# Weight sums of layer B's output blocks made in the attention passes, and two smaller moves beside them

## The chip, the cores and the metric

The kernel runs on one core of a Trainium2 chip, in one launch. The metric is the time of one execution on the device in microseconds (us), as the median of several executions. Lower is better. Five engines share the core: TensorE (PE in the profile, with PEld for its weight loads), VectorE (DVE), ScalarE (ACT), GpSimd (POOL) and SyncE (SP), which issues nearly all DMAs of this kernel. Each engine works through its own list of instructions in order, so an instruction that waits holds up all that stands behind it on that engine.

## The reference

Two layers, each with a gated attention, over a prompt of 2048 rows and a sample of 64 rows, 1024 features wide, all in float32. Layer B, the second, matters here:

```python
def gated_attention_layer(x_p, x_s, ck, cv, norm_g, w_in, q_g, k_g, w_out,
                          n_heads, n_kv, past_chunks, bias_fn, sinks):
    qp, kp, vp, gp = project(x_p, norm_g, w_in, q_g, k_g, n_heads, n_kv)
    op = prompt_band_attention(qp, kp, vp, past_chunks, bias_fn, sinks)
    y_p = x_p + (op * jax.nn.silu(gp)) @ w_out
    ...
    os_, nk, nv = sample_band_attention(qs, ks, vs, ck, cv, bias_fn, sinks)
    y_s = x_s + (os_ * jax.nn.silu(gs)) @ w_out
```

The change touches how the last product, `(op * silu(gp)) @ w_out` of layer B, gets its weights.

## The kernel before

Every float32 operand of a large product is split into a high part (rounded by ACT, `xh` or `wh`) and the rest (`xl` or `wl`, by DVE or POOL), and a product is three matmuls: high by high, high by low, low by high. A split of one 128x512 piece is therefore one ACT instruction and one DVE or POOL instruction.

The program is one long row of projection *jobs* (class `Filler`), into which the attention of both layers is woven by hand: PE's order is written out by the program. The order on the other engines and on SP is made by a scheduler that works with estimated times. Small pieces of work that nobody waits for at once (weight splits, norms) go into a queue (`Background`); it is drained a few items at a time beside the attention. When a job starts, it prefetches the activations of the next one and may start the weights of a later one (`Filler.step`).

Layer A comes first, then its output projection, then layer B in eight *passes* (two heads each, `hp` 0 to 7), each over the units 0 to 6, 8 (the sample) and 7. What follows the passes is the place of this change:

- **The direct jobs.** The first 512 rows of the layer's output are projected directly: `output_jobs(1, 1, ...)` for the right half of the columns and `output_jobs(1, 0, ...)` for the left, two jobs each of 256 rows, 96 matmuls a job. They stand beside the attention of the last units. Each job runs over four column blocks `m`; two of them share a residual tile `res` (two buffers in all), which is loaded from `x1`, added to the product by DVE (L1481) and stored to `y` (L1485). The eight weight chunks of a half come through three buffers `wraw`; each is split by ACT (L329) and DVE (L330), and the eighth of the left half into four small tiles `ev` (L739, L740).
- **The blocks.** The other 1536 rows are three blocks of 512 rows (`block_output`). Each is a 2x2 block product done with seven products instead of eight (a Strassen-Winograd scheme): products 0, 1, 2 use weights as they are, products 3 to 6 use sums of weight blocks named `t2`, `t3`, `t1` and `t4`. Each product has 48 matmuls. Product 0 is copied from PSUM to the tile `p1` by ACT (L1689), and product 1 then adds to the same PSUM banks, so PE may start product 1 only behind that copy. Between the first block's product 1 and product 2 stands the sample's output, `work(1)` and `work(0)` (L1520 to L1530).
- **The sums before.** `run` (inside `block_output`) first issues the loads of the weight blocks into tiles `R` (L1557), and makes the sums there: four DVE instructions for each of four slices `k` (L1564, L1565, L1569, L1570), twelve splits into tiles `tw` (ACT L1573, POOL or DVE L1575) and four of `t4` (ACT L1582, POOL L1583). The tiles of `block_output` lie where the attention's tiles were, so nothing of this can start before the attention's last outputs.

The operands of product `g` are made two products ahead (`operand`, splits at L1640 and L1642, sums at L1631 to L1635); the products' results are added to the residual tiles `R` by DVE and POOL (L1674).

Of the kernel before, what the change touches and what calls it, by code (L numbers as in the profile page):

```python
# [15 lines left out]
P = 128  # L16
# [35 lines left out]

DT = 256
ATTENTION = {
    "p", "ph", "pl", "q1", "G", "gt", "o1", "pa", "pb", "sq", "f", "nm", "sm", "VT", "VS",
# [4 lines left out]
def hybrid_encoder_kernel(  # L60
# [179 lines left out]
    x1 = dr.tile([P, KC, TOK], F32, tag="x1", name="x1")  # L240
    xs = dr.tile([P, 2 * KC * TOK], F32, tag="xsa", name="xsa")
    xo = dr.tile([P, 4 * NU + 1, 8 * P], F32, tag="xo", name="xo")

# [544 lines left out]
    class Filler:  # L788
# [9 lines left out]
        def step(self):  # L798
            if self.gen is None:
                self.n += 1  # L800
                if self.n >= len(self.jobs):
                    return False
                if self.n == 0:
                    self.x = self.jobs[0].prefetch()
                    self.jobs[0].weights()
                for q in self.x.items:
                    bg.run(q)
                if self.n + 1 < len(self.jobs):
                    nxt = self.jobs[self.n + 1]
                    self.x = nxt.prefetch()  # L810
                    if nxt.weights is not None:
                        nxt.weights()
                if self.n + EARLY < len(self.jobs):
                    nxt = self.jobs[self.n + EARLY]
                    if nxt.weights is not None and nxt.early:
                        nxt.weights(WP)
                self.gen = self.jobs[self.n].gen()
            c = next(self.gen, None)
            if c is None:
                self.gen = None  # L820
                return self.step()
            self.done += c
            if not self.attending:
                bg.drain(FR * c)
            return True
# [335 lines left out]
    def layer_b():  # L1161
# [226 lines left out]
        def pipeline():  # L1388
# [8 lines left out]
            filler.attending = True  # L1397
            prev = pend = None
            for x, it in enumerate(its):
                heads = [(i, h) for h in range(2) for i in range(len(it.unit[2]))]  # L1400
                c0 = filler.done
# [42 lines left out]
    def output_jobs(layer, half, xin, xout, W, count, early=True, small=-1):  # L1444
# [8 lines left out]
        def add_unit(j):  # L1453
# [9 lines left out]
            def gen():  # L1463
                oc = st.x.pop(j)
                w = st.w
                for m in range(4):
                    if m % 2 == 0:
                        c = 4 * half + m
                        res = t("res", [P, 2 * OT], 2)
                        rv = res[:, : 2 * W].rearrange("p (k s) -> p k s", k=2)  # L1470
                        load(rv, xin[:, c : c + 2, o : o + W])
                    ps = psum("pj", 512, 2)
                    for k in range(KC):
# [5 lines left out]
                        if k < KC - 1:  # L1479
                            yield 3 * W / 2400  # L1480
                    nc.vector.tensor_tensor(rv[:, m % 2], ps[:, :W], rv[:, m % 2], op=ALU.add)  # L1481
                    if "sq" in held:
                        held.pop("sq")()
                    if m % 2:
                        store(xout[:, c : c + 2, o : o + W], rv)  # L1485
                        if layer == 0:
                            held["sq"] = add_squares(half, m, o, rv)
                            if half == 1 and j == NO - 1 and m == 3:
                                held.pop("sq")()
# [8 lines left out]
        for j in range(count):  # L1498
            add_unit(j)
        return st  # L1500

    def sample_output(st, xx):
# [31 lines left out]
    def block_output(ow, pw, st):  # L1534
        LAST = (SEQ - 2 * DT) // (2 * DT)
        s = Item()
        s.A, s.R, s.x, s.T, s.q = {}, {}, {}, {}, {}

# [10 lines left out]

        def weight_raw(k):  # L1550
            q = {}
            for pair in (((1, 1), (0, 1)), ((0, 0), (1, 0))):
                r = ot("R", [P, 1024], 6)
                for e, (i, n) in enumerate(pair):
                    q[i, n] = v = r[:, 512 * e : 512 * e + 512]
                    kk = 4 * i + k
                    load(v, w_o_b[n, kk // 2, :, kk % 2, :])  # L1557
            s.q[k] = q

        def weight_sums(k):  # L1560
            q = s.q[k]
            t3, t2, t1, t4 = q[0, 1], q[0, 0], q[1, 1], q[1, 0]
            op = nc.vector.tensor_tensor
            op(t3, q[1, 1], t3, op=ALU.subtract)  # L1564
            op(t2, t2, t3, op=ALU.add)  # L1565
            if k % 2 == 0:
                s.t4 = ot("p1", [P, 1024], 3)
            keep4 = s.t4[:, 512 * (k % 2) : 512 * (k % 2) + 512]
            op(keep4, t4, t2, op=ALU.subtract)  # L1569
            op(t1, t1, t2, op=ALU.subtract)  # L1570
            for n, v in (("t2", t2), ("t3", t3), ("t1", t1)):
                w = ot("tw", [P, 2, 512], 12, F32R)
                nc.scalar.copy(w[:, 0], v)  # L1573
                e = nc.vector if n == "t2" else nc.gpsimd
                e.tensor_tensor(w[:, 1], v, w[:, 0].bitcast(F32), op=ALU.subtract)  # L1575
                s.T[n, k] = w[:, 0], w[:, 1]
            s.last = keep4

        def weight_last(k, v):
            def fn():  # L1580
                w = t("wh", [P, 1, 512], WN, F32R)[:, 0], t("wl", [P, 1, 512], WN, F32R)[:, 0]
                nc.scalar.copy(w[0], v)  # L1582
                nc.gpsimd.tensor_tensor(w[1], v, w[0].bitcast(F32), op=ALU.subtract)  # L1583
                s.T["t4", k] = w
            return fn

# [59 lines left out]
        def product(b, n):  # L1646
# [29 lines left out]
            if n == 0:  # L1676
                s.p1 = ot("p1", [P, 1024], 3)
            for h in range(2):
# [23 lines left out]
        def run(sample):  # L1702
            left = filler.total - filler.done
            later = []
            for q in filler.x.items:
                bg.run(q)
            raw(0, 0, 0)
            raw(0, 0, 1)
            for k in range(3):
                weight_raw(k)  # L1710
            work = sample(ot("sx", [P, 1024], 1, F32R))
            for k in range(4):
                if k == 1:
                    weight_raw(3)
                weight_sums(k)
                later.append(weight_last(k, s.last))
                if k == 1:
                    filler.to(filler.done + left / 2)
                    operand(0)
                    operand(1)  # L1720
                    raw(0, 1, 0)
                    raw(0, 1, 1)
            for i, j in ((0, 1), (1, 1), (1, 0), (0, 0)):
                residual(0, i, j)
            filler.to(filler.total)
            for b in range(LAST):
                for n in range(7):
                    if (b, n) == (0, 2):
                        work(1)
                        work(0)  # L1730
                        for fn in later:
                            fn()
                    product(b, n)

        return run

    with tc.manual_schedule(engines={mybir.EngineType.PE}):
# [4 lines left out]
        st = {1: output_jobs(1, 1, x1, y, DT, 2)}  # L1742
        st[0] = output_jobs(1, 0, x1, y, DT, 2, False, 7)
        with tc.tile_pool(name="pa", bufs=4, space=bass.MemoryType.PSUM) as scores_pool[0]:
# [120 lines left out]
```

## Time and profile before

| | us |
|---|---|
| median of 3 runs | 2267.66 (2266.33 to 2269.95) |
| the profiled execution, its own time | 2270.15 |
| its span in the trace | 2268.3 |

The span is what the trace covers; 1.85 us of the execution lie around it. In a row of the timeline stand the start in us, the duration in us, the engine, the line, the operation, output<-input, the shape, and in brackets how long the engine had been idle before it and which engine, tile and line ended that. A row of the windows has the stretch, its length, then for each engine busy time and number of instructions, the granted clock of TensorE as a share of full speed, the share of the 16 DMA engines and GB/s.

### The profile page before, as it was taken

The numbers are of one execution on the slowest core, as the hardware profiler recorded it, in microseconds if no ns is written. First come the engines' busy times: TensorE is split into PE (matmuls) and PEld (weight loads), VectorE is DVE, ScalarE is ACT, GpSimd is POOL, SyncE is SP. The second block draws the span as 40 slices with busy tenths as digits, with TensorE's granted clock in tenths as the row PEclk, the third lists the DMA queues.
The fourth block names the chain that finished last, engine by engine and source line by source line (L and its number), as shares of the span: only waits on it lengthen the run. The fifth ranks groups of instructions, "written<-read, shape, count | busy, mean of one in ns | idle before, by whom it ended". The sixth has DMA issues, their size and how long they took to land.

```text
span 2268.3 us, 40836 instructions
## 1 busy us (share of the span) xinstructions
PE 2222.8 (98%) x13879; PEld 1894.4 (84%) x13879; DVE 1489.6 (66%) x4232; ACT 1328.7 (59%) x3393; POOL 794.8 (35%) x1157
## 2 busy tenths in 40 slices
PE   8999999999999999999999999999999999999899
PEld 7887888888889998877888888888888888888799
DVE  7779888888785545665655655656556556565654
ACT  7888777777774335654554555555546555565311
POOL 5654533333354446332222221222212212233552
PEclk9999999999999999999999999999999999999999
DMA  8846446754446668554454544444445444444642
GB/s 273 295 149 199 157 140 195 225 185 147 149 131 199 211 192 278 182 178 141 153 146 134 160 138 154 136 145 150 146 133 159 145 145 143 145 120 140 213 139 80
DMA packets 234434, 376.91 MB, mean 166 GB/s; under 512 B 25888, under 2 KB 162480, under 8 KB 234192
## 3 DMA queue, kind: packets, MB, share of 16 engines
q1 hardware_dynamic: 234224, 374.29, 53.7%
q8 instruction: 110, 1.80, 0.3%
q14 instruction: 100, 0.82, 0.1%
HBM read 293.77 MB, written 82.08 MB: 166 GB/s over the span
## 4 chain that ended last, share of the span: by engine, by line
PE 79%; DMA 5%; issue 5%; DVE 4%; POOL 4%; ACT 2%; SPq 0%; POOLq 0%; ACTq 0%; DVEq 0%
PE pj L554 11%; PE pj L556 10%; PE pj L555 10%; PE o L1378 6%; PE sb L770 6%; PE pj L640 4%; PE pj L642 4%; PE pj L641 4%; PE sb L1302 3%; PE sb L1301 3%; PE tp L770 2%; PE sa L770 2%; PE pj L1476 2%; PE pj L1478 1%; PE pj L1477 1%
## 5 line engine op out<-in xcount | busy, mean ns | idle before, releaser
L554 PE MATMUL pj<-wh,xx 128*128 128x512 f32 x1024 | 426.3, 416 | 0.0
L556 PE MATMUL pj<-wh,xx 128*128 128x512 f32 x1024 | 403.6, 394 | 0.0
L555 PE MATMUL pj<-wl,xx 128*128 128x512 f32 x1024 | 401.7, 392 | 0.0
L1308 DVE CUSTOM_DVE_ANT_0 p<-sb,BT 128x640 f32<-128x640 f32 (+5 forms) x272 | 196.5, 722 | 179.3 <-PE sb L1302 174.9
L1312 ACT ACTIVATE p<-p,nm 128x640 f32<-128x640 f32 (+5 forms) x272 | 204.4, 752 | 186.9 <-DVE nm L1308 184.1
L681 POOL TENSOR_TENSOR f<-f,mhalf 128x4 f32<-128x4 f32 (+1 forms) x136 | 137.4, 1011 | 425.1 <-DVE f L680 425.1
L640 PE MATMUL pj<-wh,xx 128*128 128x512 f32 (+1 forms) x624 | 245.9, 394 | 1.7 <-ACT pb L662 1.1
L641 PE MATMUL pj<-wl,xx 128*128 128x512 f32 (+1 forms) x624 | 233.0, 373 | 2.5 <-DVE wl L337 2.5
L642 PE MATMUL pj<-wh,xx 128*128 128x512 f32 (+1 forms) x624 | 234.1, 375 | 0.0
L554 PEld LDWEIGHTS pj<-wh,xx 128*128 128x128 f32 x1024 | 192.7, 188 | 44.1 <-issue 20.1
L556 PEld LDWEIGHTS pj<-wh,xx 128*128 128x128 f32 x1024 | 192.2, 188 | 44.7
L555 PEld LDWEIGHTS pj<-wl,xx 128*128 128x128 f32 x1024 | 193.6, 189 | 23.6
L415 POOL TENSOR_TENSOR xx<-xraw,xx 128x528 fp32r<-128x528 f32 (+1 forms) x120 | 162.5, 1373 | 129.7 <-ACT xx L414 128.8
L662 ACT ACTIVATE pa<-pj,rms 128x384 f32<-128x384 f32 (+1 forms) x219 | 117.9, 538 | 142.8 <-PE pj L556 128.9
L1476 PE MATMUL pj<-xx,wh 128*128 128x264 f32 (+1 forms) x632 | 182.7, 289 | 3.9 <-DVE res L1481 3.9
L1477 PE MATMUL pj<-xx,wh 128*128 128x264 f32 (+1 forms) x632 | 180.0, 285 | 0.2 <-POOL xx L415 0.2
L1478 PE MATMUL pj<-xx,wl 128*128 128x264 f32 (+1 forms) x632 | 179.3, 284 | 0.5 <-DVE wl L330 0.5
L1067 ACT ACTIVATE p<-p,nm 128x257 f32<-128x257 f32 (+2 forms) x272 | 134.5, 498 | 74.6 <-DVE nm L1061 65.9
L770 PEld LDWEIGHTS sb<-ident,p 128*128 128x128 f32 x1168 | 143.0, 141 | 38.0 <-issue 4.6
L770 PE MATMUL sb<-ident,p 128*128 128x128 f32 x1168 | 172.2, 273 | 2.0 <-DVE ph L1348 1.1
L1193 POOL COPY VT<-pa 128x128 f32<-128x128 f32 x128 | 40.2, 314 | 360.8 <-ACT pa L662 360.6
L698 DVE TENSOR_TENSOR pa<-pa,f 128x256 f32<-128x256 f32 (+3 forms) x221 | 116.9, 529 | 59.9 <-POOL f L681 49.1
(324 smaller groups left out, 5907.1 us busy)
## 6 DMA issues: line engine op xcount, KB each, us to landing
xx<-xo SPq DMA_DIRECT2D x231, 512.0 KB, 3.5
xx<-xsa SPq DMA_DIRECT2D x88, 512.0 KB, 4.7
xraw<-oga SPq DMA_DIRECT2D x64, 264.0 KB, 3.4
xo<-xx SPq DMA_DIRECT2D x33, 512.0 KB, 4.6
xsa<-xx SPq DMA_DIRECT2D x32, 512.0 KB, 4.2
wraw<-in_w_in_b_dram SPq DMA_DIRECT2D x64, 256.0 KB, 3.2
xraw<-in_x_dram SPq DMA_DIRECT2D x40, 256.0 KB, 5.0
res<-in_x_dram SPq DMA_DIRECT2D x32, 264.0 KB, 2.9
```

The source lines that it names most:

```text
L554: nc.tensor.matmul(ps, xh, wh, start=k == 0, stop=False)
L555: nc.tensor.matmul(ps, xh, wl, start=False, stop=False)
L556: nc.tensor.matmul(ps, xl, wh, start=False, stop=k == KC - 1)
L640: nc.tensor.matmul(ps[:n, :C], xh, wh, start=k == 0, stop=False)
L641: nc.tensor.matmul(ps[:n, :C], xh, wl, start=False, stop=False)
L642: nc.tensor.matmul(ps[:n, :C], xl, wh, start=False, stop=k == KC - 1)
L770: nc.tensor.transpose(out, in_, ident[:n, :n])
L1308: mi = nc.vector.tensor_tensor_reduce(out=p[:n, :nk], in0=S[:n, o : o + nk], in1=bias[:n, b0 : b0 + nk], op0=ALU.add, op1=ALU.min, scale=1 ...
L1312: ex = nc.scalar.activation(p[:n, :nk], p[:n, :nk], AF.Exp, scale=-1.0, bias=nmh, accum_out=it.sm[:n, 2 * i + h : 2 * i + h + 1],)
L1476: nc.tensor.matmul(ps[:, :W], wh, oh, start=k == 0, stop=False)
L1477: nc.tensor.matmul(ps[:, :W], wh, ol, start=False, stop=False)
L1478: nc.tensor.matmul(ps[:, :W], wl, oh, start=False, stop=k == KC - 1)
```

## The change

Three things change together.

1. The sums `t2`, `t3`, `t1`, `t4` are made during passes 1 to 4 of layer B, one slice `k` in each pass, as five items for the background queue (the loads at unit 0, then one sum at units 2, 4, 6 and 8). They use the tiles `xraw` and `res`, which are idle in those passes. High and low part are stored to a DRAM tile `wt`. `run` then only loads them (`weight_load`): `t2`, `t3` and `t1` in loads of 512 KB, `t4` in loads of 256 KB.
2. The weights of the left half of the direct jobs are started two jobs ahead (`early == 2`), not one.
3. In a direct job of layer B the column blocks 2 and 3 get residual tiles of their own (`row`, one for each), so `res` serves blocks 0 and 1 alone.

```diff
+SUMS = ("t2", "t3", "t1", "t4")
...
+    wt = dr.tile([4, 4, P, 2, 512], F32, tag="wt", name="wt")
...
+                if self.n + 2 < len(self.jobs):
+                    nxt = self.jobs[self.n + 2]
+                    if nxt.weights is not None and nxt.early == 2:
+                        nxt.weights()
                 if self.n + EARLY < len(self.jobs):
                     nxt = self.jobs[self.n + EARLY]
-                    if nxt.weights is not None and nxt.early:
+                    if nxt.weights is not None and nxt.early is True:
...
+            sums = weight_sums()
             for x, it in enumerate(its):
+                if sums and it.hp > 0 and it.unit[0] % 2 == 0:
+                    bg.put(1.5, sums.pop(0))
...
-                        res = t("res", [P, 2 * OT], 2)
-                        rv = res[:, : 2 * W].rearrange("p (k s) -> p k s", k=2)
-                        load(rv, xin[:, c : c + 2, o : o + W])
+                        if m and W == DT:
+                            rv = [t("row", [P, VL], 2)[:, :W] for _ in range(2)]
+                            for k in range(2):
+                                load(rv[k], xin[:, c + k, o : o + W])
+                        else:
+                            res = t("res", [P, 2 * OT], 2)[:, : 2 * W].rearrange("p (k s) -> p k s", k=2)
+                            load(res, xin[:, c : c + 2, o : o + W])
+                            rv = [res[:, k] for k in range(2)]
...
+        def add_slice(k):
+            q = {}
+            op = nc.vector.tensor_tensor
+
+            def load_raws():
+                for i, n in ((1, 1), (0, 1), (0, 0), (1, 0)):
+                    q[i, n] = t("xraw", [P, 2 * OT], XR)[:, :512]
+                    kk = 4 * i + k
+                    load(q[i, n], w_o_b[n, kk // 2, :, kk % 2, :])
+
+            def split(n):
+                def fn():
+                    t3, t2, t1, t4 = q[0, 1], q[0, 0], q[1, 1], q[1, 0]
+                    if n == "t2":
+                        op(t3, t1, t3, op=ALU.subtract)
+                        op(t2, t2, t3, op=ALU.add)
+                    elif n == "t4":
+                        op(t4, t4, t2, op=ALU.subtract)
+                    elif n == "t1":
+                        op(t1, t1, t2, op=ALU.subtract)
+                    hi, lo = (t("res", [P, 2 * OT], 2, F32R)[:, :512] for _ in range(2))
+                    split_to(hi, lo, {"t1": t1, "t2": t2, "t3": t3, "t4": t4}[n])
+                    for e, a in enumerate((hi, lo)):
+                        store(wt[SUMS.index(n), k, :, e], a.bitcast(F32))
+                return fn
...
-            for k in range(3):
-                weight_raw(k)
             work = sample(ot("sx", [P, 1024], 1, F32R))
-            for k in range(4):
-                if k == 1:
-                    weight_raw(3)
-                weight_sums(k)
-                later.append(weight_last(k, s.last))
-                if k == 1:
-                    filler.to(filler.done + left / 2)
-                    operand(0)
-                    operand(1)
-                    raw(0, 1, 0)
-                    raw(0, 1, 1)
-            for i, j in ((0, 1), (1, 1), (1, 0), (0, 0)):
-                residual(0, i, j)
+            operand(0)
+            operand(1)
+            residual(0, 0, 0)
+            residual(0, 1, 1)
+            weight_load("t2")
+            filler.to(filler.done + left / 2)
+            raw(0, 1, 0)
+            raw(0, 1, 1)
+            residual(0, 0, 1)
+            residual(0, 1, 0)
+            weight_load("t3")
             filler.to(filler.total)
...
+            product(0, 0)
+            weight_load("t1")
+            product(0, 1)
+            work(1)
+            weight_load("t4")
+            work(0)
...
-        st[0] = output_jobs(1, 0, x1, y, DT, 2, False, 7)
+        st[0] = output_jobs(1, 0, x1, y, DT, 2, 2, 7)
```

PE's list is the same row for row, the line numbers aside. ACT's list keeps its length; its sixteen casts for the sums move from the tail into the passes. POOL's list loses its twelve splits, DVE's exchanges its tail work for 32 instructions in the passes, and SP's grows.

First, ACT in the tail, from the last operand of product 1 to the operands of product 2. `xx` are operands, `tw` and `wh` weights, `p_...` fed by `pw` is the copy of product 0, `oq` are blocks of the attention's output. Before:

```order
L1640 CAST xx_25771<-oq_25647 128x512
L1573 CAST tw_25685<-R_25649 128x512
L1573 CAST tw_25698<-R_25658 128x512
L1573 CAST tw_25701<-R_25655 128x512
L1573 CAST tw_25704<-R_25655 128x512
L1573 CAST tw_25787<-R_25664 128x512
L1573 CAST tw_25790<-R_25661 128x512
L1689 COPY p_5331_25890<-pw_25888 128x512
L1689 COPY p_5331_25890<-pw_25889 128x512
L1573 CAST tw_25793<-R_25661 128x512
L1640 CAST xx_25879<-oq_25645 128x512
```

After:

```order
L1669 CAST xx_25819<-oq_25801 128x512
L1718 COPY p_5369_25985<-pw_25983 128x512
L1718 COPY p_5369_25985<-pw_25984 128x512
L1669 CAST xx_25974<-oq_25799 128x512
L1669 CAST xx_25980<-oq_25801 128x512
```

The six casts of sums that stood between the operand and the copies are gone, and the copies follow the operand directly.

Second, ACT at the change from the first direct job to the second (L329 is L331 now, L739 is L741, L414 is L416, L1312 is L1318): `wraw` are weights of the left half as loaded, `xraw_25112` is the fourth activation piece of the second direct job, `p_25328` a score tile of the sample. Before, this stretch held no weight work:

```order
L1312 ACTIVATE p_25081,sm_24883<-p_25081,nm_24884 128x640
L1348 COPY pl_25100<-sb_25101 128x5x128
L414 CAST xx_24969<-xraw_24961 128x512
L1312 ACTIVATE p_25129,sm_25122<-p_25129,nm_25123 64x320
```

After:

```order
L331 CAST wh_25239<-wraw_25154 128x512
L331 CAST wh_25245<-wraw_25160 128x512
L1318 ACTIVATE p_25268,sm_25028<-p_25268,nm_25029 128x640
L1354 COPY pl_25299<-sb_25300 128x5x128
L331 CAST wh_25275<-wraw_25237 128x512
L741 CAST ev_25279<-wraw_25243 128x256
L416 CAST xx_25120<-xraw_25112 128x512
L741 CAST ev_25280<-wraw_25243 128x256
L1318 ACTIVATE p_25328,sm_25321<-p_25328,nm_25322 64x320
```

The weight casts moved ahead by a whole job, and the cast of the activation piece now stands behind two of them.

Third, DVE in pass 2, where the sum `t2` of slice 1 is put in (`ISA p` takes the scores out of PSUM, `COPY pl` the transposed weights of the attention). Before:

```order
L1308 ISA nm_15726 128x1
L1348 COPY pl_15709<-sb_15752 128x4x128
L679 TENSOR_REDUCE f_15736<-sq_15735 128x4
L707 SCALAR_TENSOR_TENSOR pb_15665<-sq_15742,pb_15665 128x128
L680 TENSOR_SCALAR f_15736<-f_15736 128x4
L1308 ISA p_15774,nm_15726<-sb_15769,BT 128x640
```

After:

```order
L1314 ISA nm_15771 128x1
L1537 TENSOR_TENSOR xraw_15427<-xraw_15425,xraw_15427 128x512
L1538 TENSOR_TENSOR xraw_15429<-xraw_15429,xraw_15427 128x512
L1354 COPY pl_15754<-sb_15805 128x4x128
L681 TENSOR_REDUCE f_15781<-sq_15780 128x4
L709 SCALAR_TENSOR_TENSOR pb_15710<-sq_15787,pb_15710 128x128
L742 TENSOR_TENSOR res_15793<-xraw_15429,res_15792 128x512
L682 TENSOR_SCALAR f_15781<-f_15781 128x4
L1314 ISA p_15827,nm_15771<-sb_15822,BT 128x640
```

Two sums stand ahead of the copy, and the split's rest ahead of the next scores.

On SP the order of the tail stays much as it was: the last residual load of the direct jobs waits for the store that empties its buffer, then come the attention's last store, two tiles `oq`, and behind them now two residuals `R` and the four `t2` loads, where the raw weights stood.

More of the change, by code (lines that the diff above doesn't have):

```diff
@@ L1480, in gen @@
                             yield 3 * W / 2400
-                    nc.vector.tensor_tensor(rv[:, m % 2], ps[:, :W], rv[:, m % 2], op=ALU.add)
+                    nc.vector.tensor_tensor(rv[m % 2], ps[:, :W], rv[m % 2], op=ALU.add)
                     if "sq" in held:
@@ L1484, in gen @@
                     if m % 2:
-                        store(xout[:, c : c + 2, o : o + W], rv)
+                        if m == 3 and W == DT:
+                            for k in range(2):
+                                store(xout[:, c + k, o : o + W], rv[k])
+                        else:
+                            store(xout[:, c : c + 2, o : o + W], res)
                         if layer == 0:
-                            held["sq"] = add_squares(half, m, o, rv)
+                            held["sq"] = add_squares(half, m, o, res)
                             if half == 1 and j == NO - 1 and m == 3:
@@ L1500, in output_jobs, with weight_sums @@
         return st
+    def weight_sums():
+        items = []
+        def add_slice(k):
[21 more added lines that the diff above has]
+                return fn
+            items.append(load_raws)
+            items.extend(split(n) for n in SUMS)
+        for k in range(4):
+            add_slice(k)
+        return items
     def sample_output(st, xx):
@@ L1536, in block_output @@
         s = Item()
-        s.A, s.R, s.x, s.T, s.q = {}, {}, {}, {}, {}
+        s.A, s.R, s.x, s.T = {}, {}, {}, {}
         def ot(tag, shape, bufs, dt=F32):
@@ L1548, in banks, with weight_load @@
             return [psum("pw", 512, 4, pw) for _ in range(2)]
[L1550 to L1585, printed above, removed]
+        def weight_load(n):
+            for k in range(4):
+                if n == "t4":
+                    w = t("wh", [P, 1, 512], WN, F32R)[:, 0], t("wl", [P, 1, 512], WN, F32R)[:, 0]
+                    for e in range(2):
+                        load(w[e].bitcast(F32), wt[SUMS.index(n), k, :, e])
+                else:
+                    x = ot("tw", [P, 2, 512], 12, F32R)
+                    load(x.bitcast(F32), wt[SUMS.index(n), k])
+                    w = x[:, 0], x[:, 1]
+                s.T[n, k] = w
         def columns(n, k, m):
@@ L1676, in product @@
             if n == 0:
-                s.p1 = ot("p1", [P, 1024], 3)
+                s.p1 = ot("p1", [P, 1024], 2)
             for h in range(2):
@@ L1703, in run @@
             left = filler.total - filler.done
-            later = []
             for q in filler.x.items:
@@ L1708, in run @@
             raw(0, 0, 1)
-            for k in range(3):
-                weight_raw(k)
             work = sample(ot("sx", [P, 1024], 1, F32R))
-            for k in range(4):
-                if k == 1:
-                    weight_raw(3)
-                weight_sums(k)
-                later.append(weight_last(k, s.last))
-                if k == 1:
-                    filler.to(filler.done + left / 2)
-                    operand(0)
-                    operand(1)
-                    raw(0, 1, 0)
-                    raw(0, 1, 1)
-            for i, j in ((0, 1), (1, 1), (1, 0), (0, 0)):
-                residual(0, i, j)
-            filler.to(filler.total)
[L1726 to L1733, printed above, removed]
+            operand(0)
[9 more added lines that the diff above has]
+            weight_load("t3")
+            filler.to(filler.total)
+            product(0, 0)
[4 more added lines that the diff above has]
+            work(0)
+            for g in range(2, 7 * LAST):
+                product(*divmod(g, 7))
         return run
```

## The prediction

> **What bounds the kernel now.** I read the page first, then who PE waited for from 2040 us on, then the windows.
>
> ```profile
> PE 2222.8 (98%) x13879; PEld 1894.4 (84%) x13879; DVE 1489.6 (66%) x4232; ACT 1328.7 (59%) x3393; POOL 794.8 (35%) x1157
> ...
> PE pw L1685 <- ACT p L1689: 6.7, 1, 6.7
> PE pj L1685 <- DVE R L1674: 4.8, 2, 4.1
> PE pj L1686 <- POOL xx L1642: 1.7, 1, 1.7
> PE pj L1476 <- ACT ev L739: 1.3, 1, 1.3
> PE pj L1478 <- DVE ev L740: 1.0, 1, 1.0
> PE pj L1478 <- DVE wl L330: 0.5, 2, 0.3
> ```
>
> PE is busy for 98% of the span, so no other engine's load matters by itself; time can only come out of PE's idle gaps and of matmuls that run at a lower clock. After 2040 us PE idles 16.0 us (the sum of these six rows), all but 0.7 of it at places that the change touches. The windows show what each gap costs:
>
> ```profile
> 1200.00:1371.00 171.00, 170.88 (x1018) 139.27 (x1017) 100.90 (x273) 93.88 (x241) 37.38 (x69) 1.00 0.49 147
> ...
> 2088.00:2098.00 10.00, 7.15 (x39) 6.27 (x38) 6.44 (x11) 5.70 (x12) 4.70 (x5) 0.83 0.70 196
> 2118.90:2124.90 6.00, 5.96 (x51) 5.76 (x49) 5.97 (x8) 2.18 (x4) 3.08 (x2) 1.00 1.06 384
> 2124.90:2131.50 6.60, 0.00 (x0) 0.00 (x0) 6.60 (x9) 3.39 (x7) 3.78 (x3) 0.76 0.65 237
> 2131.50:2139.00 7.50, 7.46 (x49) 7.46 (x50) 7.50 (x10) 1.09 (x2) 2.77 (x2) 0.76 0.84 244
> 2153.00:2165.00 12.00, 6.13 (x51) 5.72 (x49) 3.13 (x4) 2.00 (x4) 12.00 (x10) 1.00 0.40 101
> 2165.00:2183.50 18.50, 18.50 (x144) 18.50 (x145) 15.72 (x19) 2.90 (x5) 5.92 (x5) 0.91 0.47 138
> 2183.50:2224.10 40.60, 39.89 (x338) 39.70 (x338) 21.01 (x29) 9.76 (x17) 18.27 (x13) 1.00 0.48 142
> ```
>
> In a pass (the first row, 171 us) PE idles 0.12 us with DVE at 59% and POOL at 22%. From 2124.9 to 2131.5 PE does nothing while DVE is busy throughout: the sums. From 2153 to 2165 POOL is busy all 12 us and PE half: the splits. Behind each long gap the granted clock is low. The second block (last row) loses 0.7 us.
>
> **The change part by part.** The gain is the first block with the sample, less what it takes when nothing waits.
>
> ```profile
> 2119.02 0.28 PE L1685 MATMUL pw<-xx,wh 128*128 128x256 f32 x1
> ...
> 2138.97 0.40 PE L1520 MATMUL pj<-wh,sx 128*128 128x512 f32 x1
> ...
> 2147.21 0.36 PE L1685 MATMUL pw<-xx,wh 128*128 128x256 f32 x1
> ...
> 2177.87 0.28 PE L1685 MATMUL pj<-xx,wh 128*128 128x256 f32 x1
> ...
> 2183.55 0.28 PE L1685 MATMUL pw<-xx,wh 128*128 128x256 f32 x1
> ```
>
> Product 0 starts at 2119.02, the next block at 2183.55: 64.53 us. Undisturbed, a product takes 5.68 (product 6, the last two rows) and the sample 8.24 (2138.97 to 2147.21). Seven products and the sample are 7 x 5.68 + 8.24 = 48.0. Lost are **16.5 us**: gaps of 6.7, 1.7 and 4.1, the rest at a low clock.
>
> Does each gap go? The 6.7 is the copy of product 0, which stands on ACT behind casts of sums:
>
> ```profile
> 2129.86 1.14 ACT L1573 CAST tw<-R 128x512 fp32r<-128x512 f32 x2 [1.05 <-DVE R L1565]
> 2130.91 1.07 ACT L1689 COPY p<-pw 128x512 f32<-128x512 f32 x2
> ...
> 2105.80 0.38 SPq L1485 DMA_DIRECT2D out_dram<-res  x1
> 2110.02 0.36 SPq L1471 DMA_DIRECT2D res<-x  x1
> ...
> 2110.94 1.03 SPq L1607 DMA_DIRECT2D oq<-ogb  x2
> ```
>
> These casts are gone from there, and the copies stand right behind the last operand of product 1, so the first half is copied while PE still works on the second. POOL's splits are gone too, and with them the 1.7 and the 4.1 (a DVE addition that waited behind POOL's). Next in line are the loads. SP still waits out a store before the last residual load (4.2 us, 2105.80 to 2110.02) and then issues `oq`; I keep that wait and move all of it forward by the 4.5 us of the next part, so `oq` goes out at 2106.4. Ahead of the last operand of product 2 then stand two `oq`, two `R`, four `tw`, one `xraw`, one store and one `oq`: 4.25 MB. The fastest stretch above moved 384 GB/s; by it they land at 2117.5, by the 237 GB/s of the row below it at 2124.3. Eight DVE sums, a cast and a POOL part follow, some 8 us at the durations shown below (0.68 and 1.7): 2125 to 2132. Product 2 is due at 2119.0 - 4.5 + 2 x 5.68 + 8.24 = 2134.1. So it is in time at both ends. The `t1` loads end after 9.25 MB: by 2131 or 2145; product 5 is due at 2151. `t4` waits for `work(1)` to free its buffers (2130), then 2 MB: by 2139; due at 2157. I cost the loads at nothing; PE's own work hides them, and if that cover went, every us late is one us.
>
> The left half's weights come next. They arrived late because their loads stood on SP behind a residual load that waited for a store:
>
> ```profile
> 2077.90 0.42 SPq L1485 DMA_DIRECT2D out_dram<-res  x1
> 2082.06 0.36 SPq L1471 DMA_DIRECT2D res<-x  x1
> 2082.51 1.37 SPq L313 DMA_DIRECT2D wraw<-in_w_o_b_dram  x3
> ...
> 2091.53 0.71 ACT L739 CAST ev<-wraw 128x256 fp32r<-128x256 f32 x2
> ```
>
> A job earlier, these loads go out near 2060 and need to be split by 2087. Gone are the gaps of 1.3, 1.0 and 0.5, and the clock: 0.83 over the 10 us from 2088 to 2098 is 10 x 0.17 = 1.7 us. Together **4.5 us**.
>
> The clock piece is where a page speaks. Rows first: product 1 runs at 0.76 behind the 6.7 gap, and 0.91 over 18.5 us is another 1.7 behind the 4.1. The Trainium skill ("TensorE: Matmul & The Clock Gate", Part 1: The HAM clock gate) has the clock halve after an idle window of about 3.4 us and return after about 3.4 us of work. By that rule, the two long gaps fit, but the scattered gaps at 2088 would cost no clock, and the sum would be 19.3 instead of 21.0. The trace disagrees there: 0.83.
>
> What is added lies in passes 1 to 4: 16 loads, 32 stores, 16 casts on ACT, 32 instructions on DVE, in 16 sums. The passes have room:
>
> ```profile
> 1303.74 0.28 PE L1302 MATMUL sb<-KB,q 128*128 128x256 f32 x1
> ...
> 1309.14 0.27 PE L770 MATMUL sb<-ident,p 128*128 128x128 f32 x1
> ...
> 1304.93 0.83 ACT L1312 ACTIVATE p<-p,nm 128x640 f32<-128x640 f32 x1 [0.43 <-DVE nm L1308]
> ...
> 1306.54 0.83 DVE L1348 COPY ph<-sb 128x640 f32<-128x640 f32 x1
> ...
> 2127.48 0.68 DVE L1570 TENSOR_TENSOR R<-R,R 128x512 f32<-128x512 f32 x1
> 2128.09 1.75 DVE L1565 TENSOR_TENSOR R<-R,R 128x512 f32<-128x512 f32 x1
> ...
> 2127.60 5.04 POOL L1575 TENSOR_TENSOR tw<-R,tw 128x512 fp32r<-128x512 f32 x3 [3.33 <-ACT tw L1573]
> ```
>
> Scores end at 1304.0, their exponential at 1305.8, and PE wants it at 1309.14: 3.3 us of slack. DVE's copy of the transposed weights ends at 1307.37, and its buffer is wanted at 1309.14 too: 1.77 us. An instruction of the sums takes 0.68, and at most two stand ahead of a copy in DVE's list: 1.36. So nothing is late, unless POOL works beside it: then the same operation took 1.75. The ends are 0 and, with all 32 at 1.75, the excess over 1.77 in each of the 16 sums: 4 x 3.5 (`t2`, three instructions) + 8 x 1.7 (`t1`, `t4`) = 27.8 us. POOL is busy 22% of a pass, so the lower end is the nearer one; I take 0.5, and another 0.5 for small new waits in the tail: 1.0 back.
>
> This is a place where a page speaks against the change. The Trainium skill ("GPSIMD Engine Reference", 1. Specifications) has POOL share its way into SBUF with DVE, with contention when a DVE instruction has two inputs there, as the sums do; by it the price would be paid on both engines. The rows agree (1.75 beside POOL, and POOL at 5.04 for three), and the price by them is the 27.8 above.
>
> **Sum:** 21.0 - 1.0 = 20.0. The profiled execution took 2270.15 (span 2268.3 and 1.85 around it), so it would take 2250.2; the median of the runs is 2.5 below it, and against that the forecast is **2247.7**.
>
> **The rivals.**
>
> *The wait moves to the second direct job.* Two of the early weight casts now stand on ACT ahead of that job's fourth activation piece.
>
> ```profile
> 2060.53 0.38 SPq L1485 DMA_DIRECT2D out_dram<-res  x1
> 2064.25 0.62 ACT L414 CAST xx<-xraw 128x512 fp32r<-128x512 f32 x1 [0.36 <-PE pj L1478]
> 2069.78 0.30 PE L1476 MATMUL pj<-xx,wh 128*128 128x256 f32 x1
> wraw<-in_w_o_b_dram SPq DMA_DIRECT2D x16, 256.0 KB, 3.3
> ```
>
> The last two weight loads go out behind the store at 2060.5, once two splits have freed `wraw`, at 2062.5 by my estimate; 3.3 to land, 0.9 for two casts, 1.7 for POOL: 2068.4. PE wants the piece at 2069.78. With loads 4 us slower the stall is 2.6 and, if the clock drops, 1.7 more: 2250.3 to 2252.0.
>
> *The loads become the bound.* 8 MB of finished weights replace 4 MB of raw ones. At 138 GB/s (2165 to 2183.5, though there little was asked for) the 4.25 MB take 31 us: product 2 would start 11 us late and cost 1.7 in clock: 2260.4. At 237 GB/s nothing is late. Against it: 384 GB/s in the same place.
>
> *DVE and POOL collide in the passes*, at the copies of the transposed weights: 27.8 us back, 2267.7 - 21.0 + 27.8 = 2274.5, slower. It takes nearly all sums beside POOL: over 25.5 of the 27.8 us for slower by 0.2%. Against it: 22%.
>
> *It does not do what it says:* the copy of product 0 still comes late, because the operand ahead of it on ACT waits for `oq`. Then only the 4.5 us of the weights go: 2263.2, no change. Against it: `oq` goes out at 2106.4, 8 us ahead of product 0 (2119.0 - 4.5).
>
> **How the numbers follow.** Forecast 0.63 (2244.5 to 2250 with run-to-run spread), wait moved 0.12, loads 0.09, collision 0.08, no effect 0.04, and 0.04 for a gain above 23 us. The range 2244.5 to 2259 holds the first two and two thirds of the third: 0.81. A change of 0.2% (4.5 us) is about what a measurement of this kernel can tell from none. Faster: 0.63 + 0.12 + 0.09 + 0.04 = 0.88; same: no effect and a quarter of the collisions, 0.06; slower: 0.06.
>
> **What would show it.** In the changed profile: the copy of product 0 starts within 1 us of the end of each half; from product 0 to the second block 48 to 49 us; clock 1.00 from 2085 to the end; PE's idle in passes 1 to 4 still below 1 us each. A row of PE waiting for `tw` or `os` in the first block would show the loads; one for `xx` near 2069 the moved wait; idle at the transposes of passes 1 to 4 the collision. Wrong would be the forecast if the passes lose more than 1 us each, or if the tail finds a new wait over 3 us.

## The result, and the profile after

| | before | after |
|---|---|---|
| median of 4 runs, us | 2268.80 (2266.33 to 2271.92) | 2249.32 (2246.26 to 2250.08) |
| ratio after to before | | 0.9911, 95% interval 0.9894 to 0.9928 |
| profiled execution, us | 2270.15 | 2250.08 |

The forecast was 2247.7 with a range from 2244.5 to 2259. The change gains 19.5 us by the medians. One of the twelve executions of order_only, a kernel of the experiments below, took 7751.88 us and is left out of its median there. Who PE waited for after 2040 us is now two rows (line, tile and engine waited for: us in total, times, longest):

```profile
PE pj L1714 <- DVE R L1703: 0.6, 1, 0.6
PE sb L1307 <- DVE nm L1314: 0.3, 1, 0.3
```

The 0.6 is the wait in the second block that was 0.7 before; the 0.3, at scores of the attention (2047.8), was not in the list of before. The windows of the changed kernel, a pass first, then the left half's direct jobs, the first block and the second:

```profile
1200.00:1371.00 171.00, 170.88 (x1020) 139.35 (x1019) 104.29 (x278) 96.98 (x247) 37.49 (x70) 1.00 0.54 163
2085.00:2115.30 30.30, 30.30 (x259) 29.35 (x260) 9.40 (x19) 8.58 (x16) 11.33 (x10) 1.00 0.59 178
2115.30:2163.50 48.20, 48.20 (x381) 45.91 (x381) 30.93 (x41) 11.06 (x19) 21.73 (x14) 1.00 0.90 321
2163.50:2204.10 40.60, 40.03 (x339) 39.83 (x338) 22.06 (x31) 10.28 (x17) 17.68 (x13) 1.00 0.52 153
```

The pass still has 0.12 us of PE idle, with 3.4 us more of DVE and 3.1 more of ACT in it than before. The clock is 1.00 in every row, and PE never stops in the first block. The timeline shows the block's two ends, the copy of product 0 and the load that was to bound its start:

```profile
2115.36 0.28 PE L1714 MATMUL pw<-xx,wh 128*128 128x256 f32 x1
...
2118.40 0.59 ACT L1718 COPY p<-pw 128x512 f32<-128x512 f32 x1 [4.31 <-PE pw L1716]
2121.24 0.59 ACT L1718 COPY p<-pw 128x512 f32<-128x512 f32 x1 [2.25 <-PE pw L1716]
...
2163.43 0.28 PE L1714 MATMUL pw<-xx,wh 128*128 128x256 f32 x1
...
2106.31 0.97 SPq L1636 DMA_DIRECT2D oq<-ogb  x2
```

From product 0 to the second block it takes 48.07 us, where 64.53 stood and 48.0 was the forecast. Both copies wait for PE alone now; the second half ends on PE just ahead of 2121.24, and the rest of its time is hidden beside product 1.

Since PE's list is the same, row for row, in every kernel here, the same matmul can be looked up in two traces, and its two start times give a **lead** over before's profiled execution. The changed kernel is 2.0 us *behind* at the first matmul of the left half's weights (2087.1 before), 3.66 ahead at product 0 (2119.02 and 2115.36), 20.12 ahead at the second block (2183.55 and 2163.43) and 20.26 at the last matmul. Gains by stretch: 5.66, 16.46, 0.14. This lead is the sharpest measure below, since single times of one kernel differ by 4 us and more.

### The profile page after: what moved, and what is told of

Its sections match the earlier page's. It is cut to its first block, busy times and chain, and to the rows that moved or that the text cites. A ratio compares the mean times of both kernels' runs of the same rounds, so it can differ in the third digit from the quotient of the medians.

```text
span 2248.3 us, 40958 instructions
## 1 busy us (share of the span) xinstructions
PE 2214.5 (98%) x13879; PEld 1887.2 (84%) x13879; DVE 1489.2 (66%) x4244; ACT 1327.0 (59%) x3393; POOL 773.8 (34%) x1145
## 4 chain that ended last, share of the span: by engine, by line
PE 55%; DVE 1%; DMA 0%; issue 0%; POOL 0%; ACT 0%; POOLq 0%; DVEq 0%
PE pj L556 10%; PE pj L558 9%; PE pj L557 9%; PE o L1384 6%; PE sb L772 5%; PE sb L1308 3%; PE sb L1307 3%; PE tp L772 1%; PE pw L1714 1%; PE pw L1715 1%; PE pw L1716 1%; PE pj L1490 1%; PE pj L1491 1%; PE pj L1492 1%; PE pj L1714 1%; PE o L772 1%
## 5 line engine op out<-in xcount | busy, mean ns | idle before, releaser
L1318 ACT ACTIVATE p<-p,nm 128x640 f32<-128x640 f32 (+5 forms) x272 | 204.4, 751 | 198.2 <-DVE nm L1314 196.0
```

Source lines behind the costliest of these rows:

```text
L1318: ex = nc.scalar.activation(p[:n, :nk], p[:n, :nk], AF.Exp, scale=-1.0, bias=nmh, accum_out=it.sm[:n, 2 * i + h : 2 * i + h + 1],)
```

## The experiments

The base of the table is each kernel's lead over the one profiled execution of before, gained in each stretch. That execution took 2270.15, 1.4 to 3.0 us more than the medians of before's runs beside the experiments: 2267.11 of 11 beside again, no_early, no_row and sums_only, 2267.40 of 23 beside weights_only, order_only, sums_pool and loads_twice, 2268.79 of 18 beside the other four. So gains of the tail may stand that much above what the medians show, and medians of different sets are comparable to some 2 us only.

| kernel | median, us | ratio to before (95%) | up to the weights | left weights | first block | after it |
|---|---|---|---|---|---|---|
| changed kernel | 2249.32 | 0.9911 (0.9894 to 0.9928) | -2.0 | 5.66 | 16.46 | 0.1 |
| again | 2248.72 | 0.9913 (0.9898 to 0.9928) | -1.0 | 5.66 | 16.46 | 0.1 |
| no_early | 2253.99 | 0.9937 (0.9924 to 0.9950) | 3.9 | -0.89 | 16.46 | 0.0 |
| no_row | 2248.09 | 0.9908 (0.9893 to 0.9924) | -2.6 | 5.66 | 16.46 | 0.1 |
| sums_only | 2252.80 | 0.9937 (0.9923 to 0.9951) | -3.0 | -1.42 | 16.75 | 0.1 |
| weights_only | 2264.37 | 0.9987 (0.9977 to 0.9998) | -1.3 | 5.66 | 1.47 | 0.0 |
| order_only | 2265.27 | 0.9983 (0.9967 to 0.9999) | -0.5 | 5.66 | 0.40 | 0.1 |
| tail_dve | 2262.92 | 0.9971 (0.9960 to 0.9981) | -0.4 | 5.66 | -0.01 | 0.0 |
| unsplit | 2258.41 | 0.9960 (0.9945 to 0.9975) | 0.0 | 5.66 | 9.07 | 0.0 |
| unsplit_dve | 2254.07 | 0.9934 (0.9919 to 0.9949) | 0.6 | 5.66 | 10.20 | 0.0 |
| sums_pool | 2248.49 | 0.9914 (0.9896 to 0.9932) | -0.1 | 5.66 | 16.46 | 0.1 |
| loads_twice | 2245.94 | 0.9903 (0.9885 to 0.9920) | 1.7 | 5.66 | 16.46 | 0.1 |
| loads_late | 2252.00 | 0.9928 (0.9912 to 0.9944) | 2.6 | 5.66 | 13.89 | -3.9 |

**again** is the changed kernel unaltered.

> The changed kernel as it is, as the base of this set. Aligned matmul by matmul, the profiled execution of the changed kernel is 2.0 us later than that of before up to 2086 us, nearly all of it won and lost in layer A, and 20.3 us earlier at the end: 22.3 us gained in the tail. If the 2.0 belong to one execution, the same alignment gives another value here and the tail's 22.3 again; if the change costs layer A or the passes 2 us, it gives 2.0 again. Time: 2249 by both.

The tail gives 22.2 again, and what comes ahead of it -1.0. Over all thirteen profiles that column runs from -3.0 to +3.9, though layer A is the same code in all: it belongs to the execution. Between 1054 us and the weights alone no kernel loses more than 0.9 us, and the three that make no sums there (weights_only, order_only, tail_dve) lose 0.1, 0.3 and 0.3. So the 2.0 is not the change's.

**no_early**, **no_row** and **sums_only** take the change apart.

```diff
-        st[0] = output_jobs(1, 0, x1, y, DT, 2, 2, 7)
+        st[0] = output_jobs(1, 0, x1, y, DT, 2, False, 7)
```

> The left half's weights one job ahead again, the rest as in the changed kernel. Theory: being two jobs ahead is what removes the gaps near 2090, and all of the 5.3 us between 2089 and 2097 come back, clock included: 2254.6. Rival: the residual tiles of their own do it, because SP then has fewer stores to wait for ahead of these loads: within 1 us of the changed kernel, 2249 to 2250.

```diff
-                        if m and W == DT:
+                        if False:
...
-                        if m == 3 and W == DT:
+                        if False:
```

> All four column blocks of the direct jobs on the two tiles res again, the rest as in the changed kernel. Theory: nothing, 2249, since SP then waits some 4 us for stores ahead of the last residual loads, but the loads behind them have over 10 us of slack. Rival: the weights two jobs ahead and the block's first operands need SP free of these waits, and PE waits 2 to 6 us near 2070, 2090 or 2115: 2251 to 2255.

sums_only has both edits.

> Only the sums moved into the passes; weights one job ahead and residual tiles as before. Theory: the parts add up, so the 17 us of the first block are gained alone (8.6 at 2125 to 2132, 2.2 at 2153, 6.1 at 2161 to 2168), and the 5.3 at 2090 remain: 2254.6, the same as with the early weights alone undone. Rival: the parts need one another, since the finished weights' loads stand behind SP's waits for stores: over 2257.

All three came out as the theory has it, within 2 us: 5.3 us lost, nothing, and 4.1 lost (2254.0, 2248.1 and 2252.8 against 2248.7). By the lead no_early loses 6.6 and sums_only 6.8. The early start of the weights is worth its 5.7 us alone (it gives them in the three kernels that follow, without the sums), the residual tiles of their own are worth nothing that shows, and the parts add up within some 1 us. In no_early the windows show what returns:

```profile
2083.00:2091.00 8.00, 4.61 (x26) 3.40 (x25) 6.33 (x11) 5.87 (x12) 3.35 (x3) 0.99 0.73 213
2091.00:2098.00 7.00, 7.00 (x49) 7.00 (x49) 2.56 (x5) 1.08 (x2) 1.36 (x3) 0.77 0.43 122
```

Gaps first, then 49 matmuls in 7 us (the changed kernel has 62 there) at a clock of 0.77.

**weights_only** leaves the sums in the tail; its code is that of before with the other two edits.

> The two smaller edits without the sums: weights two jobs ahead and residual tiles of their own; the sums are made in the tail as before. Theory: the 5.3 us near 2090 are gained and the first block stays as it was, so 5.3 less than before: about 2263. Rival: the first block's gaps are set by when the raw weights and the attention's outputs arrive, not by PE, so that an earlier start only makes them longer: no gain, 2268.

**order_only** is weights_only with two slices' sums and the residual loads written behind product 0.

```diff
-            for k in range(4):
...
+            sums(0)
+            weight_raw(3)
+            sums(1)
...
+                    if (b, n) == (0, 1):
+                        sums(2)
+                        sums(3)
```

> As with the two smaller edits, and the sums of slices 2 and 3 put into the program behind product 0, so that the copy of product 0 stands on ACT behind fewer casts, while the work of the sums stays in the tail. If the gap at 2125 is a matter of ACT's order alone, its 8.6 us go and nothing else changes: 2254.5. If the work itself is what is too much (DVE and POOL are busy with it until 2165), the gap at 2125 shrinks and those at 2153 and 2161 grow by as much: 2259 to 2264.

**tail_dve** is weights_only with POOL relieved of the splits.

```diff
-                e = nc.vector if n == "t2" else nc.gpsimd
+                e = nc.vector
...
-                nc.gpsimd.tensor_tensor(w[1], v, w[0].bitcast(F32), op=ALU.subtract)
+                nc.vector.tensor_tensor(w[1], v, w[0].bitcast(F32), op=ALU.subtract)
```

> The two smaller edits, the sums all in the tail as before the change, but their low parts all on DVE, none on POOL. Theory: POOL's backlog made the waits at 2153 and 2161, and its splits beside DVE's sums stretched these from 0.68 to 1.75; without it sums and low parts are 32 x 0.68 = 22 us of DVE from 2119, so the gap at 2125 stays (the copy stands behind eight casts that need these sums) and the 8 us of the two later waits go: 2255 to 2258. Rival: the work is too much on any engine, and DVE takes POOL's place: 2262 to 2266.

The early weights give their 5.66 in all three, and the first block next to nothing: 63.05, 64.13 and 64.53 us long, where before it took 64.53 and undisturbed takes 48. PE's waits after 2040 us in order_only:

```profile
PE pj L1699 <- POOL xx L1655: 7.2, 1, 7.2
PE pw L1698 <- ACT p L1702: 3.7, 2, 2.4
PE pj L1698 <- DVE R L1687: 2.3, 2, 1.6
```

The window of the longest:

```profile
2143.80:2151.00 7.20, 0.01 (x1) 0.00 (x0) 2.39 (x4) 0.55 (x1) 7.20 (x7) 0.68 0.63 183
```

The wait for the copy, 6.7 us in before and 7.7 in weights_only, became 3.7, as the new order was to do, and 7.2 us of waiting for POOL came up some 20 us later, with POOL busy for all of it. The time, 2265.3, is above the 2259 to 2264 that were expected of too much work, and no shorter than that of weights_only. In tail_dve it is DVE that PE waits for:

```profile
PE pw L1699 <- DVE xx L1655: 6.0, 1, 6.0
PE pw L1698 <- ACT p L1702: 3.9, 1, 3.9
```

And it is DVE that is full, by the windows of tail_dve:

```profile
2117.00:2130.00 13.00, 9.06 (x63) 8.86 (x63) 13.00 (x23) 4.47 (x8) 0.00 (x0) 0.87 0.91 302
2130.00:2142.00 12.00, 10.45 (x58) 7.76 (x56) 12.00 (x12) 5.84 (x11) 9.23 (x5) 1.00 0.46 134
```

From 2117 on DVE is busy for 25 of 25 us. So for tail_dve the rival had it right (2262 to 2266; measured 2262.9): POOL's backlog was the place of the wait, not its cause. Neither this order nor the other engine buys back the work that the tail has to do between the arrival of the weights and their use; the wait that was removed returned where the next list was late.

**unsplit** keeps the sums in the passes but stores them whole, so that the tail loads half as much and splits.

```diff
-                    split_to(hi, lo, {"t1": t1, "t2": t2, "t3": t3, "t4": t4}[n])
...
+                    store(wt[SUMS.index(n), k, :, 0], {"t1": t1, "t2": t2, "t3": t3, "t4": t4}[n])
...
+                load(w[1].bitcast(F32), wt[SUMS.index(n), k, :, 0])
+                nc.scalar.copy(w[0], w[1].bitcast(F32))
+                e = nc.vector if n == "t2" else nc.gpsimd
+                e.tensor_tensor(w[1], w[1].bitcast(F32), w[0].bitcast(F32), op=ALU.subtract)
```

> The passes make the sums but store them as one float32 tile each; the tail loads 4 MB, not 8, and splits there: sixteen casts on ACT, four low parts on DVE and twelve on POOL, as before the change. Theory: the tail's price was the splits on POOL, whose 20 us beside the operands fill POOL from 2116 to 2155, so waits for POOL return near 2153 and 2161: 2251 to 2256. Rival: the price was the late raw loads and the 16 sums on DVE, which are gone: within 1 us of 2249, and keeping the weights split buys nothing.

**unsplit_dve** has `e = nc.vector` there.

> As the one with unsplit sums, and all sixteen low parts on DVE, none on POOL. DVE was busy for 22 of 39 us from 2116 to 2155 in the changed kernel, and 16 x 0.68 = 11 us come to it. Theory of POOL's backlog: any loss of the unsplit sums goes with POOL's part: 2249 to 2250. Rival: DVE's list becomes the late one, its additions to the residuals wait behind the splits: over 2252.

Without the 16 sums the block gains 9.07 of its 16.46; the other 7.4 are the price of splitting in the tail. By the medians it is 9.7 us (2258.4 against 2248.7), or 8.0 when each is taken against the before timed beside it; both are more than the 2 to 7 that the theory allowed. Half of the price, 3.6 us, is not where the theory looked. PE's waits after 2040 us in unsplit:

```profile
PE pj L1712 <- DVE R L1701: 4.1, 3, 2.0
PE pw L1712 <- ACT p L1716: 1.9, 1, 1.9
```

The 1.9 is the copy of product 0 again, at 2122: ACT's cast ahead of it waits for a sum of an operand on DVE, which stands behind the splits of `t2` there, and the clock falls behind the gap. Of the 4.1, 3.4 us lie at 2148 and 2153, where the theory has them. The windows of unsplit:

```profile
2130.00:2142.00 12.00, 12.00 (x81) 10.19 (x81) 6.65 (x9) 7.46 (x16) 12.00 (x10) 1.00 0.98 328
2142.00:2150.00 8.00, 6.23 (x53) 6.03 (x52) 2.48 (x3) 2.45 (x4) 8.00 (x7) 1.00 0.00 1
```

In its timeline, the addition at the end of that stretch:

```profile
2149.49 0.69 DVE L1701 TENSOR_TENSOR R<-pj,R 128x512 f32<-128x512 f32 x1 [4.91 <-POOL R L1701]
```

POOL is full for 20 us, DVE's addition stands behind POOL's for 4.91, and PE waits for that addition. With all splits on DVE the block gains 10.20, only 1.1 more, not all of it: PE again waits for DVE's additions (4.7 us in three waits), which then stand behind DVE's own splits, and 1.5 for the copy. PE's gaps are no shorter than in unsplit, 5.5 us in the block against 5.3; what differs is that the clock does not fall. My expectation of 2249 to 2250 for it was wrong, for the same reason as with tail_dve, and its rival (over 2252; measured 2254.1) was right.

**sums_pool** moves the passes' 32 subtractions and additions to POOL (`op = nc.gpsimd.tensor_tensor`, the low parts with it).

> The sums of the passes on POOL (subtractions, additions and the low parts, 32 instructions), no longer on DVE. In the changed kernel all 32 took 0.68 us on DVE, none beside a long POOL instruction. Theory of the collision: now each runs on POOL beside DVE's copies, and these are slowed as the tail's sums were (0.68 to 1.75); with up to 1.77 us of slack at each copy PE loses at most 1 us a sum, 16 in all, likely 2 to 6: 2251 to 2255. Rival: the passes have room for this too: within 1 us of 2249.

It is the rival's result, 2248.5. In the timeline of sums_pool a copy of transposed weights, the first row, stands right beside a sum on POOL:

```profile
1422.39 0.82 DVE L1354 COPY ph<-sb 128x640 f32<-128x640 f32 x1
...
1422.63 1.28 POOL L1542 TENSOR_TENSOR xraw<-xraw,xraw 128x512 f32<-128x512 f32 x1
```

The copy takes 0.82 as it does alone, and all five that overlap a sum for more than half their length take 0.82 or 0.83. So the copies, which read PSUM, are not slowed by POOL here.

**loads_twice** and **loads_late** were to add 8 MB of DMA to the tail's loads.

```diff
+                        load(wd[SUMS.index(n), k, :, e], wt[SUMS.index(n), k, :, e])
...
+                    load(wd[SUMS.index(n), k], wt[SUMS.index(n), k])
```

> Behind each load of finished weights the same bytes are copied once more, from one DRAM tile into another that nobody reads: 8 MB more in the stretch from 2108 to 2150, where the changed kernel moves about 390 GB/s. Theory: that stretch is full, so 8 MB add some 21 us to the last load; t4 lands near 2150 and is wanted at 2157.6, t1 near 2138 and is wanted at 2152: t4 comes 10 to 14 us late, with the clock some 12 to 16 in all: 2261 to 2265. Rival: the loads hide with much room, because the DMA engines are not the limit: within 2 us of 2249.

This said nothing on the question: the copies depend on nothing but the stores of `wt`, and the scheduler sent them as soon as those were done, in the passes (first and last start, us):

```profile
L1615 SPq DMA_DIRECT2D wd<-wt x12: 473/490/509, 1074.6 to 1600.6; - x12
```

What it shows is that 8 MB more of copies in passes 1 to 4 cost at most the 0.9 us that this kernel loses between 1054 us and the weights, and nothing that its median shows (2245.9). For loads_late the copies read what the last attention unit writes:

```diff
+                i = 4 * SUMS.index(n) + k
+                load(wd[i], og[1][:, 6:8, SEQ - 512 : SEQ])
```

> Again 8 MB more beside the loads of the finished weights, sixteen copies of 512 KB from one DRAM tile into another, but out of a part of the attention's output that is written last, so that they cannot go before 2106 us; they stand on SP among the loads of finished weights. Theory: the stretch from 2108 to 2150 is full at about 390 GB/s, so the last loads land some 20 us later, and t4 (landed near 2150, wanted at 2157.6) comes 10 to 14 us late; the operands of products 2 to 4 may come late too: 2261 to 2270. Rival: the DMA engines have room for copies beside loads: within 2 us of 2249.

The windows over the same 70 us, first of loads_late, then of the changed kernel:

```profile
2105.00:2175.00 70.00, 66.62 (x525) 63.34 (x524) 35.44 (x48) 15.07 (x27) 25.29 (x17) 1.00 1.05 387
```

```profile
2105.00:2175.00 70.00, 70.00 (x565) 67.72 (x565) 36.81 (x49) 16.38 (x28) 31.11 (x21) 1.00 0.88 301
```

And PE's waits after 2040 us in loads_late:

```profile
PE pw L1718 <- POOL xx L1674: 2.9, 1, 2.9
PE pj L1717 <- DMA wh<-wt: 1.3, 1, 1.3
```

The DMA engines are full now for 70 us, and `t4` is late, but by 1.3 us, not 10 to 14; an operand of the second block is late by 2.9, and the clock is 0.81 over the 9 us behind that gap. Together 6.6 us of lead, and 3.3 by the medians (2252.0 against 2248.7; 1.6 when each is taken against the before timed beside it). The mechanism is the one expected, but 12 to 21 us were expected of it: in the changed kernel, at 390 GB/s in the middle of the stretch, the finished weights landed 8 us or more ahead of their use, and there was room at both ends of the stretch (0.88 of the DMA engines' time over the 70 us, now all of it).

## Why the prediction was right, and which terms were off

- **The copy of product 0** (6.7 us and the low clock behind it): it went as worked out. The block is at 48.07 us against 48.0. The rival of the loads did not come: `oq` went out at 2106.31 (2106.4 in the forecast), and 8 MB more cost 6.6 us where a full queue would have cost some 20 (8 MB at 390 GB/s).
- **The second direct job**: the wait did not move there either, though it came within 1 us. The cast of the job's fourth activation piece went behind two weight casts to 2068.70; POOL's part and PE's first use of the piece in the changed kernel:

```profile
2069.45 1.31 POOL L417 TENSOR_TENSOR xx<-xraw,xx 128x512 fp32r<-128x512 f32 x1 [1.00 <-DMA res<-x]
...
2071.77 0.30 PE L1490 MATMUL pj<-xx,wh 128*128 128x256 f32 x1
```

- **POOL's splits** (1.7 and 4.1 us): gone too. The prediction named each gap's last waiter and took it for the cause. order_only and tail_dve show that this is not enough: with the waiter relieved and the work left, the block keeps 64.1 and 64.5 us. The sum came out right because the change took away all of the work at once, sums and splits.
- **The left half's weights**: 4.5 was mis-sized, 5.66 measured. I added idle time (2.8) and the clock over 10 us (1.7). Rows of before at that place show what was left out:

```profile
2089.70 0.28 PE L1477 MATMUL pj<-xx,wh 128*128 128x256 f32 x1
2090.29 0.38 PE L1478 MATMUL pj<-xx,wl 128*128 128x256 f32 x1 [0.31 <-DVE wl L330]
2091.98 0.39 PE L1476 MATMUL pj<-xx,ev 128*128 128x256 f32 x1 [1.31 <-ACT ev L739]
2092.20 0.28 PE L1477 MATMUL pj<-xx,ev 128*128 128x256 f32 x1
```

Undisturbed, such matmuls start every 0.12 us, though a row says 0.28. Between the first two starts lie 0.59 us, 0.47 lost, and the view calls 0.31 of it idle; the next start comes 1.69 later, 1.57 lost, 1.31 called idle. A gap costs about 0.2 more than its idle time, and the first matmul behind it starts its follower 0.22 later, not 0.12. Starts counted in order give the loss; idle times do not quite. Of the 5.66 us some 4.1 lie ahead of 2094.2, where the clock falls: that is the term of the gaps, taken at 2.8. The other 1.6 lie in the stretch at the low clock, taken at 1.7.
- **The passes**: 0.5 was taken, 0.1 measured (0.11 between 1054 and 2087 us), and the 0.5 for new waits in the tail was nothing but the 0.3 at 2047.8. All 32 instructions took their undisturbed time (counts, then least, median and greatest ns):

```profile
L1537 DVE TENSOR_TENSOR xraw<-xraw,xraw x4: 680/682/689, 1071.3 to 1526.0; 128x512 f32<-128x512 f32 x4
L742 DVE TENSOR_TENSOR res<-xraw,res x16: 678/682/693, 1073.6 to 1616.8; 128x512 fp32r<-128x512 f32 x16
```

- **The collision rival** did not come, and its price stays unmeasured: of the 32 instructions, 28 have no POOL instruction beside them in the changed kernel's trace, and four overlap one by 0.02 us at most. sums_pool measured something near it, DVE's own work beside sums on POOL. The copies that PE waits for read PSUM and keep their 0.82 there. An instruction with both inputs in SBUF does not:

```profile
1271.95 1.27 POOL L1542 TENSOR_TENSOR xraw<-xraw,xraw 128x512 f32<-128x512 f32 x1
...
1272.54 0.83 DVE L709 SCALAR_TENSOR_TENSOR pb<-sq,pb 128x128 f32<-128x128 f32 x1
```

In before's passes it takes 0.27 to 0.29. The Trainium skill ("GPSIMD Engine Reference", 1. Specifications) limits the contention to DVE instructions with two SBUF inputs or in a 2-port mode; sums_pool agrees, and read to the letter that sentence takes the copies off the list, which the expectation of sums_pool feared for, but leaves the sums on DVE, the prediction's rival, on it.
- **The total**: the gain of the profiled execution was forecast at 20.0 (21.0, less 1.0 given back). Measured are 22.3 in the tail, with 2.0 lost ahead of the weights, nearly all before 1054 us, which no step foresaw and which "again" and the other profiles show to be chance. That the profiled execution met its forecast to 0.1 us (2250.08 and 2250.2) is therefore luck; the steps are right to about 1 us each.
- **The median**: 2249.32 lies 1.6 above the forecast. The 2.5 us between the profiled execution and the median, taken over from before, was 0.8 in the changed kernel.

What stays open: before has one profile only, and its tail may have been up to 3 us longer than in its other executions. That would explain why weights_only gains 7.1 in the tail by the lead and 3.0 by the medians; tail_dve, with 5.7 by the lead and 5.9 by the medians of its set, does not ask for it. No second profile of before was taken.

## What to carry to other kernels

When an engine that is never idle in the long stages stalls in a short one, sum the work that the stage asks of the *other* engines between the arrival of its data and its use, before blaming the last waiter: relieving one list, by order or by engine, moved the wait and kept the time, and doing the work earlier, in a stage with room, removed it. Finish such work completely: storing the sums whole rather than split gave back 7.4 of 16.5 us, though it halved the loads of the finished weights. To measure a stretch of a few us, compare the starts of the same instruction in two traces; it showed differences of 0.1 us where the times of single runs differed by 4.

## What the hardware showed unexpectedly

The clock does not follow the length of a gap alone. Cut finely, each low clock above is a stretch of 3.41 us, or of two or three times that, at a clock of 0.50. Before's stretch near 2094 and the 3.41 us behind it:

```profile
2094.19:2097.60 3.41, 3.41 (x18) 3.41 (x17) 1.11 (x3) 0.69 (x1) 1.17 (x3) 0.50 0.87 219
2097.60:2101.01 3.41, 3.41 (x32) 3.41 (x30) 1.25 (x2) 0.39 (x1) 0.00 (x0) 1.00 0.10 33
```

With 18 matmuls in place of 32, one such stretch costs some 1.5 us of work, however long the gap was. In unsplit one gap of 1.88 us stands at 2122 and two, of 2.0 and 1.4 us, at 2148 and 2153:

```profile
2121.18:2124.59 3.41, 1.53 (x13) 1.33 (x12) 3.41 (x5) 1.81 (x4) 2.32 (x2) 1.00 1.04 382
2124.59:2128.00 3.41, 3.41 (x18) 3.41 (x18) 3.15 (x2) 0.51 (x2) 3.41 (x3) 0.50 0.87 271
...
2148.48:2151.89 3.41, 1.65 (x14) 1.65 (x15) 1.75 (x2) 0.41 (x1) 3.41 (x3) 1.00 0.00 0
2151.89:2155.31 3.42, 2.04 (x18) 1.84 (x17) 1.29 (x2) 0.00 (x0) 2.97 (x3) 1.00 0.59 153
```

The single gap brought the low clock; the two brought nothing. These rows are cut on a grid: within each of the fourteen executions, all low stretches start whole multiples of 3.41 us apart. The gap of 1.88 lies whole in one window of that grid, and of the 2.0 only 1.76 do. From 2040 us to the last matmul the fourteen traces have twelve windows behind which the clock falls from 1.00 to 0.50. PE idles for 1.88 us or more in each of them, and for 1.78 or less in every other window at the full clock. So in this tail it is PE's idle time within one window of the grid that tells. It is not a rule for the whole kernel: near 858 us the clock falls in six of the traces behind a window without idle time.

The Trainium skill ("TensorE: Matmul & The Clock Gate", Part 1: The HAM clock gate) asks for an idle window of some 3.4 us that runs freely. The grid of 3.41 us agrees; that the window must be idle throughout does not, by the 1.88 us in unsplit and by no_early, where no gap is longer than 1.1 us.
